# Rotating images by 90 degrees: two slabs turned as a pair into freed buffers, and a new store order

## The chip, the cores and the metric

The kernel runs on one core of one Trainium2 chip. The metric is device time in microseconds (us), as the median of several executions. Each profile is one execution; its span is about 1.8 us shorter than the device time of the same run.

## The reference

```python
def setup_inputs():
    batch, c, h, w = 32, 3, 256, 256
    return {"x": np.random.randn(batch, c, h, w).astype(np.float32)}

def reference(x):
    return np.rot90(x, k=-1, axes=(-2, -1)).astype(np.float32)
```

There are 96 images of 256 x 256 floats: 25.17 MB come in and the same number of bytes goes out. No arithmetic is done on them.

## The kernel before

The images are cut into 12 slabs of 2 MiB, eight images each. A slab fills one unit of SBUF, 16 KB in each of 128 partitions, and there are 12 units and no spare one. SyncE issues every DMA. VectorE turns a slab with stream transposes of 32 x 32 blocks, and the access patterns around them do the rest of the rotation. Slab n is turned into unit n-1, whose slab has been turned already; slab 0 goes to PSUM and is copied back by ScalarE at the end.

What matters for the change is the contiguous piece that one DMA packet moves. A partition holds either 16 rows of one image (16 KB contiguous in HBM, "long") or 8 rows of each of two images (two runs of 8 KB, "short"). One slab has 4096 floats per partition and its turned form has the other shape, so that each slab is long on one side only.

```python
    RL, RS = 16, 8
    I = 2
    long_st = (0, 1, 2, last - 1, last)          # stored in 16 KB pieces, loaded in 8 KB pieces
    ...
    for n in range(n_slabs):
        t_in, t_out = units[n], units[n - 1] if n else turned0
        if n in long_st:
            src = t_in.rearrange("p i (r g c) -> p c r g i", r=RS, c=RL)
            dst = t_out.rearrange("p i f -> p (i f)").rearrange("p (c k r) -> p c r k", c=RL, r=RS)[:, :, ::-1, ::-1]
            # ... two transposes of 2048 columns each
        else:
            src = t_in.rearrange("p i f -> p (i f)").rearrange("p (r g c) -> p c r g", r=RL, c=RS)
            dst = t_out.rearrange("p i (c k r) -> p c r k i", c=RS, r=RL)[:, :, ::-1, ::-1, :]
            # ... two transposes of 2048 columns each
        # ... store of slab n, in the order 1, 2, 3, ... 11; slab 0 last
```

## Time and profile before

| | before |
|---|---|
| device time, median of 3 (of 6 in the rounds beside the changed kernel) | 123.61 us (123.62) |
| span of the profiled execution | 121.7 us |
| 16 DMA engines busy, share of the span | 97.9% |
| VectorE busy | 93.0 us, 24 transposes |
| packets on the queue (640 of them completion writes, 16 for each of 40 DMAs) | 5,248 |
| last data packet ends / last completion lands / span ends | 120.50 / 120.87 / 121.7 us |

How to read it: a profile page has the span in 40 slices, with one digit for each engine and slice, in tenths of the slice. A full DMA row means that the transfers left no hole; how fast bytes move inside it is read from the GB/s. The lines themselves are shown in the prediction. Two finer readings come from the trace's packet records (start, length and size of every packet), which no view prints: the length of single packets, and the time at which each further MiB had ended (packets taken in the order of their starts, with all earlier ones ended too). The first 24 MiB are the loads, the next 24 the stores.

### The profile page before, as it was taken

How to read it: one execution, taken by the hardware profiler on the slowest of the kernel's cores; microseconds unless marked ns; L12 is line 12 of the kernel's file. 1: busy time of each engine (PE TensorE's matmuls, PEld its weight loads, DVE VectorE, ACT ScalarE, POOL GpSimd, SP SyncE). 2: the span in 40 equal slices, each digit the busy share in tenths (PEclk: the TensorE clock that was granted, in tenths of full speed). 3: DMA queues.
4: the chain of work that ended last, by engine and by line, in shares of the span. 5: the costliest groups of instructions: out<-in, count | busy, mean ns of one | idle time of the engine just before them, and what ended most of it. 6: DMA issues, size and time to landing. Idle time of an engine off the chain costs nothing.

```text
span 121.7 us, 138 instructions
## 1 busy us (share of the span) xinstructions
DVE 93.0 (76%) x24; ACT 4.9 (4%) x3; POOL 0.2 (0%) x4
## 2 busy tenths in 40 slices
DVE  0039999999999999999999999999999993000000
ACT  0000000000000000000300000000000006500000
POOL 0000000000000000000000000000000000000000
DMA  3999999999999999999999999999999999999994
GB/s 83 425 425 431 428 447 431 431 431 431 431 431 420 425 431 420 401 428 423 420 434 431 431 417 428 423 423 431 431 431 425 431 431 428 455 431 431 431 431 178
DMA packets 5248, 50.33 MB, mean 414 GB/s; under 512 B 640, under 2 KB 640, under 8 KB 640
## 3 DMA queue, kind: packets, MB, share of 16 engines
q1 hardware_dynamic: 5248, 50.33, 97.9%
HBM read 25.17 MB, written 25.17 MB: 414 GB/s over the span
## 4 chain that ended last, share of the span: by engine, by line
DMA 60%; DVE 13%; issue 7%; DVEq 3%; ACT 2%; ACTq 1%; SPq 0%
DMA u<-in_x_dram 42%; DMA out_dram<-u 18%; DVE u L89 7%; DVE u L95 7%; DVEq L132 3%; ACT u L104 2%; ACTq L132 1%; SPq L72 0%; SPq L79 0%
## 5 line engine op out<-in xcount | busy, mean ns | idle before, releaser
L95 DVE STREAM_TRANSPOSE u<-u 128x2048 f32<-128x2048 f32 x14 | 54.7, 3956 | 0.2
L89 DVE STREAM_TRANSPOSE u<-u 128x2048 f32<-128x2048 f32 x8 | 31.3, 3986 | 0.1
L89 DVE STREAM_TRANSPOSE turned<-u 128x2048 f32<-128x2048 f32 x2 | 7.1, 3586 | 8.2 <-DMA u<-in_x_dram 8.2
L104 ACT COPY u<-turned 128x2048 f32<-128x2048 f32 x2 | 3.6, 1868 | 40.5 <-DVE u L89 40.5
L104 ACT ACT_TABLE_LOAD x1 | 1.3, 1283 | 59.8 <-DMA u<-in_x_dram 59.8
L121 POOL MEMSET const-bfloat16-1.0<- 128x1 bf16 x1 | 0.1, 101 | 0.0
L121 POOL MEMSET const-uint8-127<- 128x1 uint8 x1 | 0.1, 101 | 0.0
L121 POOL MEMSET const-float32-0.0<- 128x1 f32 x1 | 0.1, 98 | 0.2 <-issue 0.2
L121 POOL MEMSET const-float32-1.0<- 128x1 f32 x1 | 0.1, 98 | 0.0
## 6 DMA issues: line engine op xcount, KB each, us to landing
u<-in_x_dram SPq DMA_DIRECT2D x18, 1024.0 KB, 19.6
out_dram<-u SPq DMA_DIRECT2D x14, 1024.0 KB, 19.6
out_dram<-u SPq DMA_DIRECT2D x5, 2048.0 KB, 23.4
u<-in_x_dram SPq DMA_DIRECT2D x3, 2048.0 KB, 15.9
```

The lines of the kernel that those rows point to most:

```text
L89: nc.vector.transpose(out=dst[:, cs], in_=src[:, cs])
L95: nc.vector.transpose(out=dst[:, cs], in_=src[:, cs])
L104: nc.scalar.copy(out=units[last][:, i], in_=turned0[:, i])
L121: nc = _bacc.Bacc("TRN2", target_bir_lowering=False, num_devices=1)
L132: with _tile.TileContext(nc) as tc:
```

## The change

The intent is to give two more slabs 16 KB pieces on both sides. If two slabs that are long on the load side are turned together, each turned partition can hold 16 output rows of either slab. That needs two free units at once. Units 3 and 7 are made one tile, so that they can be addressed as a pair; unit 7 is free once slab 7 has been turned, and unit 3 once turned slab 4 has been stored. So slab 4 is stored second, and slab 7 is loaded right after slab 3.

```diff
-    long_st = (0, 1, 2, last - 1, last)
+    long_st = (0, 1, 2, 10, 11)
+    both = (8,)
+    paired = [n + a for n in both for a in range(2)]
 ...
+    adjacent = [(3, 7), (8, 9)]                  # these units share one tile
 ...
-    for n in range(n_slabs):
+    for n in (0, 1, 2, 3, 7, 4, 5, 6, *range(8, n_slabs)):     # loads
 ...
+        elif n in paired:
+            if n not in both:
+                return
+            src = pairs[both.index(n) + 1].rearrange("p a (r g c) -> p c r g a", r=RL, c=RL)
+            dst = pairs[both.index(n)].rearrange("p i (c k r) -> p c r k i", c=RL, r=RL)[:, :, ::-1, ::-1, :]
+            parts, step = 4, RL // 4
 ...
+        if n in paired:
+            first = n if n in both else n - 1
+            for i in range(I):
+                nc.sync.dma_start(out=st_long[n, i], in_=pairs[both.index(first)][n - first :: I, i])
 ...
+    for n in range(both[0]):
+        turn(n)
+    for n in (1, 4, 2, 3, 5, 6, 7):
+        st = store(n)
+    for n in range(both[0], n_slabs):
+        turn(n)
+        store(n)
```

(Cut: the renaming of views, and slabs 3 and 4 stored whole where each was stored by two DMAs.)

More of the change, by code (lines that the diff above doesn't have):

```diff
@@ L59, with fours @@
     ld_short, ld_long, st_short, st_long = short(rows_in), long(rows_in), short(rows_out), long(rows_out)
-    pools = [ctx.enter_context(tc.tile_pool(name=f"unit{u}", bufs=1)) for u in range(n_slabs)]
-    units = [pool.tile([P, I, F], fp32, name=f"u{u}") for u, pool in enumerate(pools)]
-    psum = ctx.enter_context(tc.tile_pool(name="psum", bufs=1, space=bass.MemoryType.PSUM))
-    turned0 = psum.tile([P, I, F], fp32, name="turned0")
-    for n in range(n_slabs):
-        if n in (1, 2, last - 1):
-            ld = nc.sync.dma_start(out=units[n], in_=ld_short[n])
+    units = [None] * n_slabs
+    adjacent = [(3, 7), (8, 9)]
+    pairs = []
+    for us in adjacent + [(u,) for u in range(n_slabs) if all(u not in us for us in adjacent)]:
+        pool = ctx.enter_context(tc.tile_pool(name=f"unit{us[0]}", bufs=1))
+        held = pool.tile([P, len(us), I * F], fp32, name=f"u{us[0]}")
+        for j, u in enumerate(us):
+            units[u] = held[:, j]
+        pairs.append(held)
+    psum = ctx.enter_context(tc.tile_pool(name="psum", bufs=1, space=bass.MemoryType.PSUM))
+    turned0 = psum.tile([P, I * F], fp32, name="turned0")
+    def fours(t):
+        return t.rearrange("p (i f) -> p i f", i=I)
+    for n in (0, 1, 2, 3, 7, 4, 5, 6, *range(8, n_slabs)):
+        if n in (1, 2, 10):
+            nc.sync.dma_start(out=fours(units[n]), in_=ld_short[n])
             continue
@@ L71, with turn @@
             if n in long_st:
-                ld = nc.sync.dma_start(out=units[n][:, i], in_=ld_short[n][:, i])
+                ld = nc.sync.dma_start(out=fours(units[n])[:, i], in_=ld_short[n][:, i])
             else:
-                ld = nc.sync.dma_start(out=units[n][i::I].rearrange("p i f -> p (i f)"), in_=ld_long[n, i])
-    def store(n, t, i):
+                ld = nc.sync.dma_start(out=units[n][i::I], in_=ld_long[n, i])
+    home = [turned0] + units[:last]
+    def turn(n):
         if n in long_st:
-            return nc.sync.dma_start(out=st_long[n, i], in_=t[i::I].rearrange("p i f -> p (i f)"))
-        return nc.sync.dma_start(out=st_short[n][:, i], in_=t[:, i])
@@ L81 @@
-    for n in range(n_slabs):
-        t_in, t_out = units[n], units[n - 1] if n else turned0
-        if n in long_st:
-            src = t_in.rearrange("p i (r g c) -> p c r g i", r=RS, c=RL)
-            dst = t_out.rearrange("p i f -> p (i f)").rearrange("p (c k r) -> p c r k", c=RL, r=RS)[:, :, ::-1, ::-1]
-            pieces = 2
-            for h in range(pieces):
-                cs = slice(h * RL // pieces, (h + 1) * RL // pieces)
-                nc.vector.transpose(out=dst[:, cs], in_=src[:, cs])
-        else:
-            src = t_in.rearrange("p i f -> p (i f)").rearrange("p (r g c) -> p c r g", r=RL, c=RS)
-            dst = t_out.rearrange("p i (c k r) -> p c r k i", c=RS, r=RL)[:, :, ::-1, ::-1, :]
-            for h in range(2):
-                cs = slice(h * RS // 2, (h + 1) * RS // 2)
-                nc.vector.transpose(out=dst[:, cs], in_=src[:, cs])
-        if n in range(5, last - 1):
-            nc.sync.dma_start(out=st_short[n], in_=t_out)
-        elif n:
-            for i in range(I):
-                store(n, t_out, i)
+            src = fours(units[n]).rearrange("p i (r g c) -> p c r g i", r=RS, c=RL)
@@ new lines, in turn @@
+            dst = home[n].rearrange("p (c k r) -> p c r k", c=RL, r=RS)[:, :, ::-1, ::-1]
+            parts, step = 2, RL // 2
+        elif n in paired:
[4 more added lines that the diff above has]
+            parts, step = 4, RL // 4
+        else:
+            src = units[n].rearrange("p (r g c) -> p c r g", r=RL, c=RS)
+            dst = fours(home[n]).rearrange("p i (c k r) -> p c r k i", c=RS, r=RL)[:, :, ::-1, ::-1, :]
+            parts, step = 2, RS // 2
@@ new lines, in turn, with store @@
+        for h in range(parts):
+            nc.vector.transpose(out=dst[:, h * step : (h + 1) * step], in_=src[:, h * step : (h + 1) * step])
+    def store(n):
+        if n in paired:
+            first = n if n in both else n - 1
+            for i in range(I):
+                nc.sync.dma_start(out=st_long[n, i], in_=pairs[both.index(first)][n - first :: I, i])
+        elif n in long_st:
+            for i in range(I):
+                nc.sync.dma_start(out=st_long[n, i], in_=home[n][i::I])
+        else:
+            return nc.sync.dma_start(out=st_short[n], in_=fours(home[n]))
@@ L103 @@
+    for n in range(both[0]):
[5 more added lines that the diff above has]
+        store(n)
     for i in range(I):
-        nc.scalar.copy(out=units[last][:, i], in_=turned0[:, i])
-    for i in range(I):
-        store(0, units[last], i)
+        nc.scalar.copy(out=fours(units[last])[:, i], in_=fours(turned0)[:, i])
+    home[0] = units[last]
+    store(0)
 _INS = ['x']
```

## The prediction

> **What bounds the kernel now.** I read the page's totals and its 40 slices first, then the stage windows, then the waits of the issuing queue, then the timeline, and last the packet records, which the page only sums up.
>
> ```profile
> DVE 93.0 (76%) x24; ACT 4.9 (4%) x3; POOL 0.2 (0%) x4
> ...
> DVE  0039999999999999999999999999999993000000
> ...
> DMA  3999999999999999999999999999999999999994
> ...
> q1 hardware_dynamic: 5248, 50.33, 97.9%
> HBM read 25.17 MB, written 25.17 MB: 414 GB/s over the span
> ```
>
> The DMA row is full in every slice but the first and the last, and the queue's packets fill 97.9% of 16 engines over the span of 121.7 us (0.979 x 121.7 = 119.1 us). VectorE is nearly as busy, but it starts two slices late and ends seven slices early. So the bound is the bytes: 25.17 MB in and 25.17 MB out, back to back. Only three things can move the time: the rate while the engines are full, a hole in the full stretch, and the two ends.
>
> The windows give the rate by stage. Columns: window, its length, busy time of VectorE, ScalarE and GpSimd, clock, DMA share, GB/s. In order they are 8 KB loads, 16 KB loads, 8 KB loads again, 8 KB stores and 16 KB stores.
>
> ```profile
> 2.76:15.02 12.26, 6.87 (x2) 0.00 (x0) 0.00 (x0) 1.00 1.01 426
> 22.44:49.36 26.92, 26.78 (x8) 0.00 (x0) 0.00 (x0) 1.00 1.01 428
> 54.26:59.22 4.96, 4.92 (x3) 0.00 (x0) 0.00 (x0) 1.00 1.01 421
> 76.39:103.35 26.96, 25.05 (x7) 1.77 (x2) 0.00 (x0) 1.00 1.01 428
> 108.33:118.06 9.73, 0.00 (x0) 0.00 (x0) 0.00 (x0) 1.00 1.00 429
> ```
>
> The stages differ by under 2%, and 8 KB stores and 16 KB stores by one GB/s. A window counts a whole packet at its edge, so I took the finer number from the packet records. One 8 KB packet lasts 309 ns in the median (3,078 of them, six of which belong to no data transfer of this kernel), one 16 KB packet 611 ns (1,536). Counted by when each further MiB had ended, an 8 KB store stretch (76.39 to 103.35 us, 11 MiB) takes 2.450 us per MiB and a 16 KB one (108.33 to 118.06 us, 4 MiB) 2.434 us.
>
> The waits of the issuing queue (SPq), in the stretch 60 to 95 us, tell whether the engines depend on anything else there:
>
> ```profile
> SPq L98 <- DVE u L95: 14.0, 3, 7.4
> SPq L98 <- DMA out_dram<-u: 7.5, 4, 2.1
> SPq L78 <- DVE u L89: 7.4, 1, 7.4
> ```
>
> The queue does wait for VectorE, up to 7.4 us at a time, yet the DMA row has no hole there: the stores issued earlier still hold the engines. The chain that ended last runs through these VectorE lines too, as far as the copy at 101.58 us, but it follows releases and not full engines. The last store is issued at 105.8 us and the last data packet ends at 120.5 us, so some 15 us of transfers are queued at that point. The chain is not the limit.
>
> **What the Trainium skill says.** "DMA: Bandwidth & Descriptors", section "Bandwidth", puts the ceiling of the ports at 435 GB/s. The trace agrees: 428 and 429 GB/s in full stretches, 1.4% under it, so there is nearly nothing to win from a better rate. The same page, in "Why small descriptors are slow", gives each packet a fixed cost of about 3 cycles. The trace agrees in sign and size: two 8 KB packets are 618 ns and one 16 KB packet 611 ns, 7 ns apart. "SBUF — State Buffer", section "SBUF: two separate sides", says that engine accesses do not slow DMA; here the 8 KB stores run at 428 GB/s with VectorE at 25.05 of 26.96 us and the 16 KB stores at 429 with VectorE idle, which fits.
>
> **The change, part by part.**
>
> 1. Packets. Slabs 3 to 9 are loaded in 16 KB pieces and stored in 8 KB pieces. Slabs 8 and 9 now leave in 16 KB pieces: 4 MiB, in 256 packets instead of 512. At 2.450 against 2.434 us per MiB that is 4 x 0.016 = 0.064 us. The bare packet lengths bound it from above: 256 x 7 ns / 16 engines = 0.11 us. This lies wholly on the path, as the engines are full. It is 0.05% of 123.61 us. DMA instructions stay at 40 (21 loads and 19 stores), so completion writes stay at 640.
>
> 2. VectorE. The instruction order shows 24 transposes of 2048 columns before and after. The pair's four take the place of two for slab 8 and two for slab 9, with the same inner shape 4x16x16x2. I charge them 3.97 us each, as L89 (3.99) and L95 (3.96) differ by 1%. The sum stays at 93 us. The new strides of 16 KB between the two slabs could cost something; part 4 says how much would be hidden.
>
> 3. Loads. Slab 7 is loaded before slabs 4 to 6, because slabs 3 and 7 now share one tile and the transpose of slab 3 waits for both loads. With 2 MiB every 4.89 us after a start near 2.8 us, slab 7 is there at 27.3 us plus a few tenths; the transpose of slab 3 starts at 31.0 us. Slab 4 now lands near 32.6 us and is wanted near 38.8 us. Neither waits.
>
> 4. The new dependence. The pair is written over units 3 and 7, and unit 3 holds turned slab 4 until that is stored. So store 4 goes second. It is issued near 47.4 us, after its transpose (31.0 + 2 x 7.85 = 46.7 us). It is behind 24 MiB of loads (done at 62.0 us) and 2 MiB of store 1, so its own 2 MiB end at 71.6 us, landing at about 72.0 (the second store in the kernel before landed at 71.97). The transposes of slabs 0 to 7 end at 70.15 us. I expect VectorE to wait about 1.8 us, and to finish the pair at 72.0 + 4 x 3.97 = 87.9 us. In the kernel before, store 8 was ready at 85.9 and store 9 at 93.7 us; now both are ready at 87.9. The stores ahead (1, 4, 2, 3, 5, 6, 7) hold the engines until 96.0 us, so 8 us of reserve remain.
>
> 5. The end. Transposes of slabs 10 and 11 end near 95.8 and 103.7 us (93.7 and 101.6 before), the copy of slab 0 near 107.4 us (105.2 before). The stores before them hold the engines until about 105.7, 110.6 and 115.5 us. The reserves are 9.9, 6.9 and 8.1 us. The added wait of 1.8 us is hidden everywhere. The last store is still slab 0 in 16 KB pieces, so the tail stays as it is.
>
> 6. Switches between sizes. The stores go 16, 8, 16, 8, 16 KB where they went 16, 8, 16. From 71.58 to 110.76 us the old kernel has one switch each way around 14 MiB of 8 KB stores; 14 x 2.450 + 2 x 2.434 = 39.17 us against 39.18 measured. A switch costs nothing that I can see.
>
> Sum: 123.61 - 0.06 = 123.55 us, with nothing taken off or put on for the ends.
>
> **The rivals.**
>
> (a) A hole in the DMA stream: the pair comes too late. For it: all four transposes must be done before either store begins, and the pair waits for store 4. Against it: it would take over 8 us of delay, for instance transposes of 6 us in place of 3.97. At 5.7 us each the pair would end at 94.8 us, still in time for itself, but the two slabs after it would come 7 us later and meet their 6.9 us of reserve. Worst case I can construct: 2 to 4 us more, 126 to 127 us. I give it about 2%.
>
> (b) 16 KB on both sides is worth more than the rate of one side shows, by something that the separate stages do not show. Against it: loads and stores hardly overlap, each stage is already within 2% of the port ceiling, and 4 MiB at the full 435 GB/s would save at most 0.16 us. The time would be 123.45 us.
>
> (c) The boundary between loads and stores moves. The 8 KB loads of slabs 10 and 11 run at 421 GB/s, and the six MiB from 51.81 to 66.71 us take 14.90 us, 0.2 over what their parts give at the rates of other stretches (4 x 2.452 + 2 x 2.434 = 14.68). With another store second, this could grow or shrink by a like amount: 123.3 to 123.8 us. Nothing in the profile says which way.
>
> **Range and chances.** The centre is 123.55 us. The three runs of before spread over 0.16 us; rival (c) adds 0.2 either way, and executions agree within 0.3%, 0.37 us. The range that should hold 8 times in 10 is 123.25 to 123.85 us. Two per cent is 2.5 us: to be faster by that, the bytes would have to go over the port ceiling, 0.5%. To be slower takes rival (a), 1.5%. Within 2%: 98%.
>
> **What would show it right or wrong.** Right: 256 data packets fewer (4,992 on the queue), the DMA row again all nines, 429 GB/s in the stretch of stores 8 and 9, one new VectorE wait of about 2 us near 70 us with a DMA store of the outputs as its releaser, VectorE done near 103.7 us, and the last data packet within 0.3 us of 120.5. Wrong: a slice of the DMA row below nine between 60 and 118 us (rival a), pair transposes well over 4 us, or a start or end that differs, the one thing that I took over unexamined.

## The result, and the profile after

The changed kernel took 123.38 us in the median (123.31 to 123.92, 6 runs), the kernel before 123.62 us (123.48 to 123.73) in the same rounds. The ratio is 0.9989, with a 95% interval of 0.9971 to 1.0008. A ratio here is the mean time of one kernel's fast runs over that of the other's of the same rounds, so it is not quite the ratio of the medians quoted. The result is correct. The two kernels cannot be told apart from this alone; the predicted time, 123.55 us, is 0.17 us above the median and the range holds it.

The profiled execution happened to be the slowest of the six (123.92 us, span 122.1). These are lines of its page, answering to those of the kernel before:

```profile
DVE 91.8 (75%) x24; ACT 4.9 (4%) x3; POOL 0.2 (0%) x4
...
DVE  0039999999999999999999929999999996000000
...
DMA  4999999999999999999999999999999999999993
...
q1 hardware_dynamic: 4992, 50.33, 97.9%
HBM read 25.17 MB, written 25.17 MB: 412 GB/s over the span
```

The queue has 256 packets fewer and the DMA row is again full. VectorE has one new gap (the 2), of which the DMA row shows nothing. The stage windows of the same execution, with the columns as in the prediction, in order: 8 KB loads, 16 KB loads, 8 KB loads again, 8 KB stores, the last 3 MiB of slabs 8 and 9 (new: 16 KB) with the first of slab 10, and later 16 KB stores.

```profile
2.66:14.92 12.26, 6.71 (x2) 0.00 (x0) 0.00 (x0) 1.00 1.01 422
22.46:49.38 26.92, 26.78 (x8) 0.00 (x0) 0.00 (x0) 1.00 1.01 428
54.13:59.10 4.97, 4.93 (x3) 0.00 (x0) 0.00 (x0) 1.00 1.01 422
81.53:93.78 12.25, 12.21 (x4) 0.00 (x0) 0.00 (x0) 1.00 1.01 429
98.77:108.51 9.74, 4.00 (x2) 3.63 (x2) 0.00 (x0) 1.00 1.01 431
108.51:118.25 9.74, 0.00 (x0) 0.00 (x0) 0.00 (x0) 1.00 1.01 431
```

By the packet records, a MiB of slabs 8 and 9 takes 2.434 us and a MiB of the 8 KB stores 2.450 us, as in the kernel before. The two longest waits of the issuing queue from 60 to 95 us and, last, the one new wait of VectorE:

```profile
SPq L119 <- DVE u L113: 16.4, 1, 16.4
SPq L124 <- DVE u L113: 5.0, 1, 5.0
```

```profile
DVE u L113 <- DMA out_dram<-u: 2.4, 1, 2.4
```

SyncE's queue now waits 16.4 us in one piece for the pair (7.4 us was the longest before), and VectorE waits 2.4 us for store 4 to land. Neither shows in the DMA row: the pair was ready at 87.1 us, and the stores ahead of it held the engines until about 96.

Why is this execution 0.5 us slower than its five sisters? The windows from 59 to 62 us, where the last loads meet the first stores, in the kernel before, in this execution and in the second profile of the changed kernel (`a_again` below):

```profile
59.00:62.00 3.00, 3.00 (x1) 1.28 (x1) 0.00 (x0) 1.00 1.03 429
```

```profile
59.00:62.00 3.00, 3.00 (x1) 1.28 (x1) 0.00 (x0) 1.00 1.01 371
```

```profile
59.00:62.00 3.00, 3.00 (x1) 1.28 (x1) 0.00 (x0) 1.00 1.04 434
```

At 371 GB/s those 3 us move 0.42 us too little of what 431 would (3 x 60 / 431; an estimate, as a window counts whole packets). In the packet records, 36 packets of 8 KB took over 330 ns there, up to 698 ns, where 309 is the median. In the kernel before it was 6. In two more profiles of the changed kernel it was 6 (`a_again`) and 15 (`a_third`), with executions of 123.48 and 123.32 us. So this is not a fixed property of the changed kernel; it differs from one execution to the next. Nor does the number of slow packets alone set the time: `a_third`, with 15, was faster than `a_again`, with 6.

The time at which each MiB had ended shows the loss in two steps. After 25 MiB this execution was 0.17 us behind `a_again` (64.54 us against 64.37), and its last MiB took 2.73 us in place of 2.45. Eight of its last 16 packets ended from 120.61 to 120.98 us, the others by 120.37. That would fit about half of the DMA engines having been held up at the turn and ending late; the records do not name the engine, so it is not shown.

### The profile page after: what moved, and what is told of

Same layout as the page of the kernel before. It is cut to its first block, busy times and chain, and to the rows that moved or that the text cites. A ratio compares the mean times of both kernels' runs of the same rounds, so it can differ in the third digit from the quotient of the medians.

```text
span 122.1 us, 135 instructions
## 1 busy us (share of the span) xinstructions
DVE 91.8 (75%) x24; ACT 4.9 (4%) x3; POOL 0.2 (0%) x4
## 4 chain that ended last, share of the span: by engine, by line
DMA 55%; DVE 16%; issue 6%; DVEq 3%; SPq 3%; ACT 2%; ACTq 1%
DMA u<-in_x_dram 35%; DMA out_dram<-u 21%; DVE u L113 16%; DVEq L163 3%; ACT u L135 2%; SPq L93 1%; ACTq L163 1%; SPq L87 1%; SPq L91 1%; DVEq L113 0%; SPq L124 0%
## 5 line engine op out<-in xcount | busy, mean ns | idle before, releaser
L113 DVE STREAM_TRANSPOSE u<-u 128x2048 f32<-128x2048 f32 x22 | 84.7, 3922 | 2.7 <-DMA out_dram<-u 2.4
```

The costliest lines, as they stand in the source:

```text
L113: nc.vector.transpose(out=dst[:, h * step : (h + 1) * step], in_=src[:, h * step : (h + 1) * step])
```

## The experiments

There were two questions. First, what makes the small gain: the size of the packets (my theory), the order of loads and stores (rival 1), or the 8 KB loads at the turn from loads to stores (rival 2)? Second, is the pair really hidden by some 8 us of stores already issued, and would the order 1, 4, 2, 3 be needed for that? Each call put its kernels on one chip beside the kernel before: first call 123.51 us for it, second 123.45, third 123.57. Every edit below is against the changed kernel.

| label | median us (runs) | ratio to before, 95% interval | last completion, then to the end, us |
|---|---|---|---|
| `a_again` | 123.43 (5) | 0.9989, 0.9977 to 1.0002 | 120.88, 0.82 |
| `no_pair` | 123.69 (5) | 1.0011, 0.9998 to 1.0024 | 120.96, 0.94 |
| `two_pairs` | 123.43 (5) | 0.9990, 0.9976 to 1.0003 | 120.90, 0.85 |
| `plain_order` | 126.18 (4) | 1.0212, 1.0198 to 1.0226 | |
| `all_16k_out` | 123.44 (5) | 1.0005, 0.9991 to 1.0019 | 120.72, 1.01 |
| `out_4k` | 125.64 (4) | 1.0179, 1.0165 to 1.0193 | |
| `pair_plus2` | 123.48 (4) | 1.0004, 0.9990 to 1.0018 | 120.91, 0.81 |
| `pair_plus4` | 130.48 (1) | one look | |
| `a_third` | 123.37 (6) | 0.9990, 0.9974 to 1.0007 | 120.72, 0.81 |
| `no_pair_40` | 123.62 (6) | 1.0013, 0.9998 to 1.0027 | 120.79, 0.81 |
| `all_16k_48` | 123.57 (6) | 0.9997, 0.9979 to 1.0015 | 120.48, 0.81 |
| `start_two_queues` | 123.29 (5) | 0.9983, 0.9969 to 0.9997 | 120.69, 0.81 |

The last column is from the one profiled execution of each.

### The changed kernel again, and the pair undone

`a_again` and `a_third` have no edit.

> The changed kernel once more, unchanged. Theory (packets): the gain is that of 256 fewer data packets, 0.06 to 0.11 us, so about 123.5 us against 123.6. Rival (turnaround): the time is set by how many 8 KB load packets are slowed where loads end and stores begin (36 of them in the first profile of this kernel, 6 in the kernel before); then a profile with few slow ones has a span near 121.5 us and one with many near 122.1 us.

> The changed kernel a third time, as the measure for the other three of this call: 123.4 us, its last completion near 120.88 us and the end near 121.65 us in the trace, 0.77 us later.

Both repeat the ratio of the first measurement: 0.9989, 0.9989 and 0.9990 in three sets of rounds. Each interval includes 1, but three sets on the same side make a gain of about 0.1%, 0.13 us, likely.

`no_pair` keeps the new order and the shared tiles and undoes the pair; slabs 8 and 9 are then stored by one DMA each in place of two:

```diff
-    paired = [n + a for n in both for a in range(2)]
+    paired = []
```

> The new load order, shared tiles and store order 1, 4, 2, 3, 5, but slabs 8 and 9 turned one by one and stored in 8 KB packets, 5,248 packets as before. Theory (packets): as the kernel before, 123.6 us, 0.06 to 0.11 us above the changed kernel. Rival (order): as the changed kernel, 123.4 us, since the order alone would have made the gain.

It took 123.69 us, 0.26 us above `a_again` beside it. (Its queue had 5,216 packets and not the 5,248 expected: 38 DMAs have 32 completion writes fewer than 40.) The order alone makes no gain, so rival 1 falls. But 0.26 us is more than packets should cost, and the trace says where part of it is. The last completion lands 0.08 us later than in `a_again`, which is what the packets should cost. The rest of the difference in the two profiles comes after the last data: 0.94 us to the end in place of 0.82. At the end, SyncE runs through the completion semaphores of eight DMAs in a fixed order, in five instructions some 0.065 us apart. With 40 DMAs the last one to complete is also the last in that order. `no_pair` has 38 DMAs, so the last completion is found at the third instruction and two more have to be run through.

`no_pair_40` tests that. It is `no_pair` with slabs 8 and 9 stored by two DMAs each, which makes 40 again (cut: `paired = []`, as above):

```diff
+            if n in (8, 9):
+                for i in range(I):
+                    nc.sync.dma_start(out=st_short[n][:, i], in_=fours(home[n])[:, i])
+                return
```

> As no_pair, but slabs 8 and 9 are each stored by two DMAs of 1 MiB, so that there are 40 DMAs again and the last of them uses the eighth completion semaphore, the one waited for last at the end. Theory (no_pair's 0.26 us over the changed kernel are 0.08 of packets and 0.11 of five waits that still had to be run through after its last completion, 0.87 us to the end in place of 0.77): 0.06 to 0.11 us above the changed kernel, near 123.5 us. Rival (the pair itself is worth 0.26 us): 123.69 us as before.

In the trace it does what the theory says: 0.81 us from the last completion to the end (the expectation counts this end a little differently, as 0.77), and a last completion 0.07 us after that of `a_third`. In the times it doesn't: 123.62 us, 0.25 us above `a_third`, as much as `no_pair` was. The six executions of `no_pair_40` run from 123.39 (the profiled one) to 123.88 us, and those of `a_third` from 123.23 to 123.81. So the worth of the pair is 0.07 to 0.08 us in the traces and 0.25 us in the medians, twice. Which of the two is the better number is open. Both kernels with the pair undone also lie above the kernel before (1.0011 and 1.0013, both intervals just reaching 1), so a part of the 0.25 us may be a cost of the new order that the pair more than makes up; that is not settled either.

### Packets of other sizes

`all_16k_out` stores slabs 3 to 7 in 16 KB pieces too. Its output is wrong, which doesn't matter for the time.

```diff
-            return nc.sync.dma_start(out=st_short[n], in_=fours(home[n]))
+            for i in range(I):
+                nc.sync.dma_start(out=st_long[n, i], in_=home[n][i::I])
```

> Wrong result on purpose: slabs 3 to 7 are stored in 16 KB packets too, as if they had been turned as pairs, so all 24 MiB of stores go out in 16 KB packets (5 slabs, 640 packets fewer than the changed kernel, no switches of size). Theory (rate only: 0.016 us per MiB): 10 x 0.016 = 0.16 us under the changed kernel, near 123.27 us. Rival (each slab with 16 KB on both sides brings more than its rate, as the 0.26 us between no_pair and the changed kernel for 4 MiB hints): 0.65 us under it, near 122.8 us.

It took 123.44 us, no less than the kernel before. In the trace the last completion landed 0.16 us before that of `a_again` (on another chip). That is the size reckoned, but by luck: after 25 MiB, before any 8 KB store had been replaced, this execution was already 0.26 us ahead (64.12 us against 64.37), from there to the last data packet it gained 0.04 us, and its last completion landed late, 0.49 us after the last data in place of 0.35. Then 1.01 us remained: with 45 DMAs the last completion is found at the second of those five instructions. `all_16k_48` mends that by loading slabs 1, 2 and 10 with two DMAs each, 48 in all. It also changes the source view of the transposes of slabs 3 to 7, which is taken up further down (cut: the slices of these two transposes).

```diff
+            for i in range(I):                       # the same stores as all_16k_out; loads of 1, 2, 10:
+                nc.sync.dma_start(out=fours(units[n])[:, i], in_=ld_short[n][:, i])
 ...
-            src = units[n].rearrange("p (r g c) -> p c r g", r=RL, c=RS)
+            src = fours(units[n]).rearrange("p i (r g c) -> p c r g i", r=RS, c=RL)
```

> Wrong result on purpose. As all_16k_out, with slabs 1, 2 and 10 loaded by two DMAs each, so that there are 48 DMAs and the last uses the eighth completion semaphore; and the transposes of slabs 3 to 7 read and write in steps of 64 bytes, which is off the path. Theory (its last completion was 0.16 us earlier than the changed kernel's, as reckoned, and 0.17 us were given back in the waits after it): 0.16 us under the changed kernel, near 123.25 us. Rival (the 16 KB packets bring nothing in the end): 123.44 us again. On VectorE: theory (a transpose is slow where one side has steps of 32 bytes in SBUF) 3.6 to 3.7 us in slabs 3 to 7; rival (the pair's 3.68 us come from the 16 KB between its two slabs) 3.95 us.

In the trace, 0.81 us after the last completion, which landed 0.24 us before that of `a_third`; from the 25th MiB to the last data packet it took 0.16 us less than `a_third`, which is the size reckoned, and every MiB of stores from 66.6 to 117.7 us took 2.434 us. That profiled execution took 123.08 us, the shortest. Its five other executions took 123.41 to 123.82, so the median, 123.57 us, misses the expected 123.25. The packets' part is seen in the trace, and in the median it is lost among differences between executions that are twice its size.

`out_4k` stores everything in 4 KB pieces, to make a cost per packet large enough to see (a wrong result; cut: the lines of the old stores):

```diff
+    st_4k = rows_out.rearrange("(n p i h r) w -> n p i h (r w)", p=P, i=I, h=2, r=RS // 2)
 ...
+        held = home[n] if n not in paired else units[{8: 3, 9: 7}[n]]
+        for i in range(I):
+            nc.sync.dma_start(out=st_4k[n][:, i], in_=held.rearrange("p (h i f) -> p i h f", i=I, h=2)[:, i])
```

> Wrong result on purpose: all stores in 4 KB packets (6,144 of them). Theory (a fixed cost per packet, 0.0041 us per packet on its engine, worked out from 2.450 and 2.434 us per MiB): a 4 KB store stretch takes 2.483 us per MiB, the whole is 1.0 us above the changed kernel, near 124.4 us. Rival (no cost per packet at these sizes, the difference seen is something else): 123.4 to 123.6 us.

It took 125.64 us: the sign is right and the rival falls, but it is twice the size expected. From 66.74 to 94.14 us a MiB took 2.490 us, near the 2.483 reckoned from a fixed 0.0041 us per packet. From about 97 us on it took 2.57 us. The windows of the two stretches:

```profile
66.74:94.14 27.40, 25.12 (x7) 0.00 (x0) 0.00 (x0) 1.00 1.03 421
104.24:119.72 15.48, 0.00 (x0) 1.91 (x2) 0.00 (x0) 1.00 1.02 407
```

The second stretch accounts for about 0.9 us (10 MiB x 0.087). The 45 DMAs of this kernel add 0.2 at the end as in `all_16k_out`. What slows the second stretch I don't know; VectorE has no transpose in the window shown. The order in which the pieces lie in HBM changed with their size, and no run separates the two.

### No 8 KB loads at the turn

`two_pairs` makes slabs 10 and 11 a second pair, so they are loaded in 16 KB pieces too. It is correct.

```diff
-    long_st = (0, 1, 2, 10, 11)
-    both = (8,)
+    long_st = (0, 1, 2)
+    both = (8, 10)
-    adjacent = [(3, 7), (8, 9)]
+    adjacent = [(3, 7), (8, 9), (10, 11)]
-        if n in (1, 2, 10):
+        if n in (1, 2):
```

> Slabs 10 and 11 made a second pair, turned into the units of 8 and 9, so that they are loaded in 16 KB packets too; no 8 KB loads are left where loads give way to stores. Theory (packets): 256 packets fewer, 4 MiB from 2.485 to 2.447 us, 0.15 us faster than the changed kernel, near 123.25 us. Rival (turnaround): the slow 8 KB load packets there are gone altogether and the gain is 0.3 us or more, 123.1 us or less. Slab 10 is then ready near 101.9 us against 105.8 us, when the stores before it end, so no hole is expected.

It has 240 packets fewer than `a_again` and the same median, 123.43 us, so rival 2 falls, and my 0.15 us did not come either. The loads of slabs 10 and 11 did become faster, 2.45 us per MiB in place of 2.485. In the two profiles that made up for a slower start: `two_pairs` was 0.10 us behind after 20 MiB (51.86 us against 51.76) and level after 25 (64.37 in both). Doing away with the 8 KB loads did not smooth the turn: there, 16 KB packets took up to 924 ns.

### How much is hidden

`plain_order` keeps the pair and stores slab 4 fourth:

```diff
-    for n in (1, 4, 2, 3, 5, 6, 7):
+    for n in (1, 2, 3, 4, 5, 6, 7):
```

> The pair, but stores in the order 1, 2, 3, 4, 5. Store 4 then lands near 82 us, the pair ends near 82.0 + 4 x 3.68 = 96.7 us, and the stores queued before it end near 96.1 us. Theory (the second place of store 4 is what hides the pair): a hole of about 2 us near 96 us and a smaller one before slab 11 (ready near 112.4 us), 125.5 to 127 us. Rival (the order does not matter, the queue holds enough): 123.4 us.

It took 126.18 us, inside the 125.5 to 127 expected. VectorE waits for store 4 until 82.02 us (11.9 us in place of 2.4), the stores of the pair are issued at 96.42 us, and the queue had run dry. Its VectorE and DMA rows:

```profile
DVE  0039999999999999999999500069999999990000
...
DMA  3999999999999999999999999999997799996995
```

Those two 7s and the later 6 are what a real loss looks like here. By the packet records, the 39th MiB took 4.18 us in place of 2.43 and the 45th, before slab 11, 3.40.

`pair_plus2` and `pair_plus4` do two or all four of the pair's transposes twice:

```diff
-            nc.vector.transpose(out=dst[:, h * step : (h + 1) * step], ...)
+            for again in range(2 if n in both and h < 2 else 1):      # pair_plus4: without "and h < 2"
+                nc.vector.transpose(out=dst[:, h * step : (h + 1) * step], ...)
```

> Two of the pair's four transposes done twice, 7.4 us of VectorE more. Theory (reserve of 8 to 9 us before a hole): the pair ends near 94.5 us, the stores before it near 96.1, no hole there; slab 11 is ready near 110.2 us against 110.8, where a hole of up to 1 us may open, so 123.4 to 124.4 us. Rival (VectorE is on the path, as the chain of waits draws it): 7.4 us longer, 130.8 us.

> All four transposes of the pair done twice, 14.7 us of VectorE more. Theory (reserve): the pair ends near 101.8 us, the stores before it near 96.1 us; a hole of 5.7 us and 1.5 us to start again, then small ones before slabs 11 and 0, so about 131 us. Rival (VectorE on the path): 138 us. Rival (the reserve is larger than reckoned): 123.4 us.

With 7.2 us more on VectorE (98.9 us busy in place of 91.7) the time stayed at 123.48 us; the 45th MiB, before slab 11, took 2.54 us in place of 2.43, so the reserve was nearly used up there, as expected. With 14.3 us more (106.0) it was 130.48 us in the one run made, 7.0 above the kernel before beside it: about half of the added work is hidden. Their VectorE and DMA rows, first with two and then with four:

```profile
DVE  0039999999999999999999939999999999990000
...
DMA  3999999999999999999999999999999999999994
```

```profile
DVE  0049999999999999999997699999999999991000
...
DMA  3999999999999999999999999999970399997995
```

VectorE can be busy until four slices before the end, as in the first, and cost nothing. So the chain of waits, which gives VectorE 13% and more of the span in both kernels, is not what bounds them.

### Two queues at the start

In the profiles the first MiB ends at 5.1 to 5.3 us though data begins at 1.75, about 0.95 us longer than a usual later MiB. `start_two_queues` loads the second half of slab 0 from ScalarE's queue:

```diff
+                q = nc.scalar if n == 0 and i == 1 else nc.sync
+                ld = q.dma_start(out=fours(units[n])[:, i], in_=ld_short[n][:, i])
```

> An attempt at a faster kernel: the second half of slab 0 is loaded from ScalarE's queue, beside the first half. In the profiles the first MiB ends at 5.1 to 5.2 us though data begins at 1.75 us, 0.95 us longer than a later MiB. Theory (the start lacks descriptors): the first MiB ends up to 0.3 us earlier and the kernel takes 123.1 us. Rival (the first packets are slow by themselves, up to 1.2 us each): no gain, 123.4 us.

It is correct and took 123.29 us, with a ratio to the kernel before of 0.9983 (0.9969 to 0.9997): the only correct kernel whose interval lies wholly below 1. Against `a_third` beside it, 123.37 us, it is not told apart. In the trace the sixteenth data packet starts at 1.93 us, where it was 2.31 in `a_third`, but the first MiB ends no sooner (5.25 us against 5.14) and the last data packet ends at 120.35 us against 120.38. So the packets start sooner and the end hardly moves; the 0.3 us hoped for did not come.

## Why the prediction was right or wrong

**Bound.** Right. `pair_plus2` shows that 7 us of VectorE work cost nothing, `plain_order` and `pair_plus4` that a hole in the DMA row costs time, and `out_4k` that a lower rate in a full row does. (A slip in the reading: VectorE's row ends six slices early and not seven.)

**Part 1, packets.** Right in mechanism, and in size as far as the traces go. The nearness of the predicted time shows little: no change at all would have been in the range too. The new 16 KB stores run at 2.434 us per MiB, as assumed; against the two kernels with the pair undone, the last completion came 0.07 and 0.08 us earlier, where 0.064 to 0.11 was said. Counted from the end of the 25th MiB to the last data packet, which leaves out the start and most of the turn, the stores took 56.22 us in the kernel before, 56.25 and 56.22 with the pair undone, and 56.16 and 56.14 in `a_again` and `a_third`. The measured ratios put the gain over the kernel before at about 0.13 us, and the medians over the kernels with the pair undone at 0.25 us. So the sum may lack a second term of 0.05 to 0.2 us, whose cause is not settled; all three intervals against the kernel before still include the predicted ratio (123.55 / 123.61 = 0.9995). That the trace agrees with the page cited there in size too is not shown: the prediction turns no cycles into ns, and its two measures differ (7 ns from packet lengths, 4 ns from the rates).

**Part 2, VectorE.** The count was right, the size was not: the pair's transposes took 3.68 us each, not 3.97. The kernel before, and the pair's four in the changed kernel (window 72:87.05):

```profile
L95 DVE STREAM_TRANSPOSE u<-u 128x2048 f32<-128x2048 f32 x14 | 54.7, 3956 | 0.2
L89 DVE STREAM_TRANSPOSE u<-u 128x2048 f32<-128x2048 f32 x8 | 31.3, 3986 | 0.1
```

```profile
L113 DVE STREAM_TRANSPOSE u<-u 128x2048 f32<-128x2048 f32 x4 | 14.4, 3683 | 2.4 <-DMA out_dram<-u 2.4
```

`all_16k_48` narrows down why. On line 114 it has the transposes of slabs 3 to 7 with a changed source view, two halves 8 KB apart and steps of 64 bytes on both sides:

```profile
L117 DVE STREAM_TRANSPOSE u<-u 128x2048 f32<-128x2048 f32 x12 | 45.7, 3883 | 4.7 <-DMA out_dram<-u 4.5
L114 DVE STREAM_TRANSPOSE u<-u 128x2048 f32<-128x2048 f32 x10 | 36.5, 3702 | 0.2
L117 DVE STREAM_TRANSPOSE turned<-u 128x2048 f32<-128x2048 f32 x2 | 7.1, 3585 | 8.1 <-DMA u<-in_x_dram 8.1
```

The ten on line 114 take 3.70 us (line 117's twelve mix the pair with the `long_st` form), so the 16 KB between the pair's slabs are not the reason. What the slow forms have in common (3.96 and 3.99 us) is a step of 8 floats, 32 bytes, on one side in SBUF: for the `else` branch it is the source, for `long_st` the destination. With the destination in PSUM, the latter takes 3.59 us. But another thing goes with the step: in both slow forms the side with 32 bytes has 32 such steps in a row, where the fast forms have 16 on each of two halves, on both sides. No run separates the step from this shape, and I tried no third step. The error was worth 1.1 us, all off the path.

**Part 3, loads.** Right: no transpose waits for a load after the first.

**Part 4, the new dependence.** Right: a wait of 2.4 us (2.2 in `a_again`) where 1.8 was said, and the pair ready at 87.1 us, where 87.9 was said, as the faster transposes more than made up for it. The reserve of 8 us held 7.2 us of added work and not 14.3.

**Part 5, the end.** Right for the last three slabs. It left out that the end after the last completion depends on the number of DMAs. Both kernels have 40, so it came to nothing here; with 38 or 45 it is 0.12 or 0.2 us, more than the effect under study.

**Part 6, switches.** Not seen to cost anything: `a_again`, with two more switches than the kernel before, ended its last data at 120.53 us against 120.50.

**Rival (a)** did not come; `plain_order` made it come, in the size given (2.6 us). **Rival (b)**, something more than the rate, is neither shown nor ruled out by the 0.25 us above. **Rival (c)** is the one that did happen, in an execution: a slow turn from loads to stores goes with a last data packet 0.48 us later in the first profiled run than in the kernel before (120.98 us against 120.50). So one of the signs that the prediction gave for being right, the last data packet within 0.3 us of 120.5, failed in that execution; in `a_again` and `a_third` it held (120.53 and 120.38). That the slow packets made all of the 0.48 us is argued and not shown.

## What to carry to other kernels

When transfers fill the span, look for the queue's reserve before counting an engine's work: how long the transfers already issued will last when the next one becomes ready. Here about 8 us of stores hid a new wait, a longer transpose step and 7 us of needless work, and an order that took that reserve away cost 2.6 us. Here 16 KB in place of 8 KB packets for 4 MiB were worth 0.07 to 0.25 us of 123, and 4 KB packets for all stores cost 2.2 us, some 0.2 of it by the number of DMAs. A gain of a tenth of a per cent needs the trace, because executions of one kernel differ by more.

## What the Trainium skill lacked or had wrong

- "DMA: Bandwidth & Descriptors", "Why small descriptors are slow": its fixed cost per packet, put at 0.0041 us from the 8 and 16 KB stores (2.450 and 2.434 us per MiB), nearly gives the first 4 KB stores (2.490 us per MiB, where 2.483 was reckoned), but not the later ones (2.57 us). The section has the cost in cycles and names no clock for them.
- The same page, as far as I read it, says nothing of the turn from loads to stores in one queue: 8 KB packets of 309 ns took up to 698 ns there and 16 KB packets of 611 ns up to 924, with 6 to 36 slow packets in three executions of one kernel.
- "VectorE: DVE Perf Modes", "The three transpose paths", gives no cost of the access pattern: 2048 columns of float32 took 3.96 to 3.99 us where one side in SBUF steps by 32 bytes, 3.68 to 3.70 us with 64 bytes on both, and 3.59 us into PSUM; whether the step or the shape of the pattern does it is open. Where the skill speaks of 16-byte lines in SBUF it gives no duration either.
- No page that I read has the program's own end: 0.81 to 1.01 us from the last completion to the end of the span, by the place of the last DMA among eight completion semaphores.
